# 512 weight columns as the moving side, k outermost, in the output projection and the second feed-forward product of a two-layer hybrid block

## The chip, the cores and the metric

The kernel runs on one core of one Trainium2 chip. The metric is the time of one execution in device microseconds (us).

## The reference, cut to what matters

Two layers work on 256 latent tokens `x` and 256 context tokens `xc`, with 1024 features. In each layer three token mixers (gated linear attention, differential attention, latent attention) share one input projection and are merged with gates into `y`; then come an output projection, a residual with a layer norm, and a SwiGLU feed-forward with another residual and norm. The context tokens are needed in layer 0 only. What matters here:

```
y = sum over branches of sigmoid(gate) * (branch @ w_branch)
y = y @ w_out                                   # 1024 x 1024
x = layer_norm(ALPHA * x + g1 * y) * ln1_g + ln1_b
h = layer_norm(x) * (1 + sc2) + sh2
gate, up = split(h @ ffn_w_in)                  # 1024 x 5632
f = (silu(gate) * up) @ ffn_w_out               # 2816 x 1024
x = layer_norm(ALPHA * x + g2 * f) * ln2_g + ln2_b
```

The shifts, scales and gates (sh, sc, g; six per layer) come from `silu(c) @ w_mod[l]`, which the kernel computes in steps between its other work.

## The kernel before, in words

All matrices are float32. To get float32 accuracy from TensorE, each operand is split into a rounded high part and a remainder, and one product takes three matmuls (mm3, lines 233 to 236): high by high, then the two mixed ones. A weight tile is loaded into a `raw` slot of up to 1024 elements a partition (load, line 181, on SP's queue; four slots), and split (line 198) in pieces of 512 elements a partition: ScalarE writes the high part (line 212), VectorE the remainder (line 213). Both go into `wh` and `wl`, three slots each, or into `wo`, 33 slots, where a tag is given and the weights are held. Loads and splits have high priority in the planner.

A planner orders each engine's instructions: it simulates the program with a cost model and takes, by priority, what is ready; program order gives the priority. On the chip each engine then follows that fixed order and waits on semaphores.

Tokens stand in tiles of 128, i = 0 and 1 latent, 2 and 3 context. In layer 0, NT = 4 tiles, in the last layer NT = 2.

**The output projection** (lines 1164 to 1185). The merged mixer output XM has eight tiles M (features on partitions), made by merge (line 967) in the order n = 0 to 7; hilo writes the high part on ScalarE (line 514) and the rest on VectorE (line 515). Tokens are taken in groups: (0, 1) and (2, 3) in layer 0, (0) and (1) in layer 1. Per group there are four blocks cb_ of 256 columns; per block and tile, tok_block goes through k = 0 to 7 with the token tile of XM as the stationary side and 256 weight columns as the moving side, 24 matmuls into one accumulator. The first group loads and holds all weights (16 splits), the second goes through the blocks backwards. After each block and tile proj_res (line 1157) multiplies by the gate row (line 1159), adds to the residual (line 1160) and takes statistics (line 1162), all on VectorE. After a group, residual (line 980) and modulate (line 374) make X2, by VectorE, TensorE transposes (line 384) and ScalarE (line 388); mods_until forces outstanding modulation steps. Just before, gate_rows (line 354) fetches the gate row on ScalarE's queue (line 410), which has to wait until the row's store (line 331) has landed.

**The feed-forward** (lines 1190 to 1261). hidden makes one of 22 tiles u, features on partitions, from ffn_w_in. In layer 0 this is done in two rounds, tiles 0 to 11 and 12 to 21 (RND = 12), and the first NLAT = 4 tiles of the first round are made for tokens 0 to 255 before tokens 256 to 511. After each round the second product adds into the residual: four blocks cb_ of 256 columns, per block an accumulator per token tile, k (here f) outermost in steps of four and the tiles inside. In layer 0's second round the tiles are taken in two parts, (0, 1) and (2, 3), each followed by residual and modulate for layer 1's X; the second part goes backwards through the blocks and keeps the weights of the last block (FHELD = 1). In layer 1 all 22 k are one round; its last block goes tile by tile, so that the first tile's residual and store run beside the second tile's matmuls.

**The modulation steps.** tick (line 338) counts; on every third tick it closes an open row and does one mod_step (line 289): a 512 KB load of w_mod, 16 matmuls, and with every fourth step a ScalarE copy of the row. wfeat, wtok, branch_part and mla_front_pass tick; the loop of the second product doesn't. Channel 5 of the last layer isn't taken by ticks.

Of the kernel before, what the change touches and what calls it, by code (L numbers as in the profile page):

```python
# [11 lines left out]
ALU = mybir.AluOpType  # L12
# [3 lines left out]
P = 128  # L16
D = 1024
KD = D // P
# [13 lines left out]
ALPHA = (2 * DEPTH) ** 0.25  # L32
# [11 lines left out]
def hybrid_block_kernel(  # L44
# [6 lines left out]
    nc = tc.nc  # L51
# [7 lines left out]
    def nm(s):  # L59
        uid[0] += 1  # L60
        return f"{s}_{uid[0]}"
# [3 lines left out]
    def T(shape, tag, dtype=F32):  # L65
        return sb.tile(shape, dtype, tag=tag, name=nm(tag), bufs=BUFS[tag])
# [3 lines left out]
    NEARLY = 8  # L70
    NCHAIN = 24
    NLAT = 4
    HELD = 4
    FHELD = 1
    RND = 12
    PB = dict(mm=8, s=2, t=2, o=6, md=1, first=15)

    def ps(tag, shape):
        return pp.tile(shape, F32, tag="ps_" + tag, name=nm("ps_" + tag), bufs=PB[tag])
# [34 lines left out]
    mm = nc.tensor.matmul  # L114
    act = nc.scalar.activation
    stt = nc.vector.scalar_tensor_tensor
    tt = nc.vector.tensor_tensor
# [21 lines left out]
    cur = []  # L139
# [58 lines left out]
    def split(v, tag=None):  # L198

        a, b = v.shape[1], v.shape[2]  # L200
        step = a if a * b <= 512 else a // 2
        hs, ls = [], []
        with tc.high_priority():
            for o in range(0, a, step):
                n = step * b
                if tag:
                    h, lo = T([P, 512], tag, F32R), T([P, 512], tag, F32R)
                else:
                    h = wp.tile([P, 512], F32R, tag="wh", name=nm("wh"), bufs=WB)
                    lo = wp.tile([P, 512], F32R, tag="wl", name=nm("wl"), bufs=WB)  # L210
                h, lo = [t[:, 0:n].rearrange("p (k c) -> p k c", c=b) for t in (h, lo)]
                nc.scalar.copy(h, v[:, o:o + step, :])  # L212
                tt(lo, v[:, o:o + step, :], r32(h), op=ALU.subtract)  # L213
                hs += [h[:, k, :] for k in range(step)]
                ls += [lo[:, k, :] for k in range(step)]
        return hs, ls

    def wtile(src, kt, n, tag=None):
        return split(load(src, kt, n), tag)
# [13 lines left out]
    def mm3(o, lh, ll, rh, rl, start, stop):  # L233
        mm(o, lh, rh, start=start, stop=False)  # L234
        mm(o, lh, rl, start=False, stop=False)  # L235
        mm(o, ll, rh, start=False, stop=stop)  # L236
# [13 lines left out]
    def wtok(src, tag=None):  # L250

        tick()
        tick()
        return [wtile(src[512 * j:512 * j + 512, :], 4, 256, tag) for j in range(2)]

    def tok_block(o, ws, X, t0, c0, c1):

        k = 0
        for wh, wl in ws:
            for j in range(len(wh)):  # L260
                mm3(o, X[k][0][:, t0:t0 + P], X[k][1][:, t0:t0 + P], wh[j][:, c0:c1], wl[j][:, c0:c1],
                    k == 0, k == KD - 1)
                k += 1
# [74 lines left out]
    def tick():  # L338
        ticks[0] += ticking[0]
        if ticking[0] and ticks[0] % ticks[1] == 0:  # L340
            if mod_open:
                mod_close()
            if mod_queue and (mod_now or mod_queue[0] < (DEPTH - 1, 5, 0)):
                mod_step()
# [690 lines left out]
    X, copied, ahead = first_X()  # L1035
# [29 lines left out]
    for l in range(DEPTH):  # L1065
# [10 lines left out]
        g = keep([P, 6])  # L1076
# [5 lines left out]
    for l in range(DEPTH):  # L1082
        last = l == DEPTH - 1
        TQ = L if last else L + LC
        NT = TQ // P
        if l:
            X = Xn
# [61 lines left out]
        XM = [pair("M", TQ) for n in range(KD)]  # L1149
# [5 lines left out]
        gw = [gate_rows(l, 2, s) for s in range(NT // 2)]  # L1155

        def proj_res(i, po, c0, gw, r, a, st=None):
            tmp = T([P, 512], "rt")[:, 0:256]
            tt(tmp, po, gw[i // 2][c0 // 512][:, c0 % 512:c0 % 512 + 256], op=ALU.mult)
            stt(r[:, c0:c0 + 256], r[:, c0:c0 + 256], a, tmp, op0=ALU.mult, op1=ALU.add)  # L1160
            if st is not None:
                nc.vector.bn_stats(st[:, c0 * 6 // 256:c0 * 6 // 256 + 6], r[:, c0:c0 + 256])

        X2 = new_X(TQ)
        groups = [(0,), (1,)] if last else [(0, 1), (2, 3)]
        wo = {}
        st = {i: small(24) for i in range(NT)}
        for g in groups:
            for cb_ in range(4) if g is groups[0] else (3, 2, 1, 0):

                if cb_ in wo:
                    ws = wo[cb_]
                else:
                    held = g is groups[0] and cb_ >= 4 - (4 if last else HELD)
                    ws = wtok(w_out[l, :, 256 * cb_:256 * cb_ + 256], "wo" if held else None)
                    if held:
                        wo[cb_] = ws
                for i in g:
                    po = ps("mm", [P, 256])
                    tok_block(po, ws, XM, P * i, 0, 256)  # L1180
                    proj_res(i, po, 256 * cb_, gw, cur[i], ALPHA, st[i])
            mods_until(l, 4)
            for i in g:
                residual(l, i, cur[i], G1, B1, st[i])
                modulate(cur[i], i, l, 3, X2)
        mods_until(l, 5)
        gw2 = [gate_rows(l, 5, s) for s in range(NT // 2)]
# [14 lines left out]
        for lo_f, hi_f in (((0, RND), (RND, 22)) if TQ == 512 else ((0, 22),)):  # L1202
            u = {f: pair("u", TQ) for f in range(lo_f, hi_f)}
            jobs = [(f, 0, TQ) for f in range(lo_f, hi_f)]
            if lo_f == 0 and TQ == 512:
                jobs = [(f, a, a + 256) for a in (0, 256) for f in range(NLAT)] + jobs[NLAT:]
            for f, a, b in jobs:
                hidden(f, a, b, *u[f])
            final = hi_f == FT
            parts = [range(NT)] if not final or last else [range(0, 2), range(2, 4)]  # L1210
            if final:
                st = {i: small(24) for i in range(NT)}
                if not last:
                    mods_until(l + 1, 1)
            held = {}
            for part in parts:
                for cb_ in range(4) if 0 in part else (3, 2, 1, 0):
                    tags = [t for t in ("mm", "t", "s", "o") for _ in range(PB[t])][4 * (cb_ % 2):]
                    pos = {i: ps(tags[n], [P, 256]) for n, i in enumerate(part)}

                    keeps = len(parts) > 1 and cb_ >= 4 - FHELD
                    ws = held.setdefault(cb_, {}) if keeps else {}

                    def ffn_out(f0, i, tag="wo" if keeps else None):
                        kt = min(4, hi_f - f0)
                        if f0 not in ws:
                            ws[f0] = wtile(ffn_w_out[l, P * f0:P * (f0 + kt), 256 * cb_:256 * cb_ + 256], kt, 256, tag)
                        wh, wl = ws[f0]
                        for f in range(f0, f0 + kt):
                            mm3(pos[i], u[f][0][:, P * i:P * i + P], u[f][1][:, P * i:P * i + P],  # L1230
                                wh[f - f0], wl[f - f0], f == lo_f, f == hi_f - 1)

                    steps = range(lo_f, hi_f, 4)
                    if last and cb_ == 3:

                        for i in part:
                            for f0 in steps:
                                ffn_out(f0, i, "wo")
                    else:
                        for f0 in steps:  # L1240
                            for i in part:
                                ffn_out(f0, i)
                    for i in part:
                        proj_res(i, pos[i], 256 * cb_, gw2, cur[i], 1.0 if lo_f else ALPHA,
                                 st[i] if final else None)
                if not final:
                    continue
                for i in part:
                    residual(l, i, cur[i], G2, B2, st[i])
                    if last:  # L1250
                        for j in range(2):
                            q = nc.sync if j else nc.scalar
                            q.dma_start(out[0, P * i:P * i + P, 512 * j:512 * j + 512], cur[i][:, 512 * j:512 * j + 512])
                    else:
                        if i == 0:
                            Xn = new_X(512)
                        if i < 2:
                            mid = tc.dram_tile([P, D], F32, name=f"mid{i}")
                            nc.scalar.dma_start(mid, cur[i])
                            tok[i] = mid  # L1260
                        modulate(cur[i], i, l + 1, 0, Xn)
# [53 lines left out]
```

## Time and profile before

| | |
|---|---|
| median of 3 runs | 2120.98 us (2118.11 to 2122.21) |
| profiled execution, its own time | 2119.53 us |
| its span in the trace | 2117.7 us |
| mean granted TensorE clock | 0.992 |
| busy: TensorE matmul, VectorE, ScalarE, GpSimd | 97%, 69%, 51%, 5% of the span |
| from HBM | 263.79 MB, 126 GB/s over the span |

The page gives busy time by engine over the whole span; matmuls are pipelined, so their busy times overlap, and what one costs in a stream is read from start to start. The page's chain, followed back from the last instruction, lies on TensorE for 77% of the span, on VectorE for 12% and on ScalarE for 5%.

### The profile page before, as it was taken

The numbers are of one execution on the slowest core, as the hardware profiler recorded it, in microseconds if no ns is written. First come the engines' busy times: TensorE is split into PE (matmuls) and PEld (weight loads), VectorE is DVE, ScalarE is ACT, GpSimd is POOL, SyncE is SP. The second block draws the span as 40 slices with busy tenths as digits, with TensorE's granted clock in tenths as the row PEclk, the third lists the DMA queues.
The fourth block names the chain that finished last, engine by engine and source line by source line (L and its number), as shares of the span: only waits on it lengthen the run. The fifth ranks groups of instructions, "written<-read, shape, count | busy, mean of one in ns | idle before, by whom it ended". The sixth has DMA issues, their size and how long they took to land.

```text
span 2117.7 us, 36478 instructions
## 1 busy us (share of the span) xinstructions
PE 2052.3 (97%) x14103; PEld 1808.8 (85%) x14103; DVE 1461.3 (69%) x3240; ACT 1073.1 (51%) x2495; POOL 98.2 (5%) x187
## 2 busy tenths in 40 slices
PE   7999999999999999899999999999999999998998
PEld 4888887887878788798899889988988988998998
DVE  4599758778478766685443348598577888785655
ACT  3755446666465642344321233765466676644452
POOL 0001001111000000010000000000011000000000
PEclk9999999999999999999999999999999999998999
DMA  9332333332322344646334346533434333668653
GB/s 292 100 90 80 116 85 113 89 107 71 101 72 75 82 140 124 183 120 182 95 98 137 114 125 188 149 94 115 142 90 141 108 114 87 177 203 212 167 176 115
DMA packets 349271, 268.30 MB, mean 127 GB/s; under 512 B 19932, under 2 KB 316520, under 8 KB 349096
## 3 DMA queue, kind: packets, MB, share of 16 engines
q1 hardware_dynamic: 335632, 252.22, 41.4%
q10 hardware_dynamic: 13464, 13.74, 2.2%
q8 instruction: 111, 1.82, 0.4%
q14 instruction: 64, 0.52, 0.1%
HBM read 263.79 MB, written 2.12 MB: 126 GB/s over the span
## 4 chain that ended last, share of the span: by engine, by line
PE 77%; DVE 12%; ACT 5%; issue 2%; POOL 2%; DMA 1%; ACTq 0%; DVEq 0%; POOLq 0%; SPq 0%
PE ps_mm L234 18%; PE ps_mm L235 18%; PE ps_mm L236 18%; PE ps_s L234 3%; PE ps_s L236 3%; PE ps_s L235 3%; POOL store L178 2%; DVE wl L213 2%; PE ps_md L299 2%; PE ps_s L682 1%; ACT rt L483 1%; PE ps_s L509 1%; PE ps_s L510 1%; PE ps_o L786 1%; ACT wh L212 1%
## 5 line engine op out<-in xcount | busy, mean ns | idle before, releaser
L213 DVE TENSOR_TENSOR wl<-raw,wh 128x512 fp32r<-128x512 f32 (+2 forms) x719 | 468.4, 674 | 143.1 <-ACT wh L212 70.7
L212 ACT CAST wh<-raw 128x512 fp32r<-128x512 f32 (+2 forms) x719 | 416.4, 611 | 234.7 <-PE ps_mm L235 128.8
L234 PE MATMUL ps_mm<-X,wh 128*128 128x512 f32 (+1 forms) x1264 | 438.9, 347 | 0.0
L236 PE MATMUL ps_mm<-X,wl 128*128 128x512 f32 (+1 forms) x1264 | 434.2, 344 | 0.0
L235 PE MATMUL ps_mm<-XL,wh 128*128 128x512 f32 (+1 forms) x1264 | 434.1, 343 | 0.0
L234 PEld LDWEIGHTS ps_mm<-X,wh 128*128 128x128 f32 x1264 | 241.3, 191 | 30.4 <-issue 4.7
L236 PEld LDWEIGHTS ps_mm<-X,wl 128*128 128x128 f32 x1264 | 240.9, 191 | 24.8
L235 PEld LDWEIGHTS ps_mm<-XL,wh 128*128 128x128 f32 x1264 | 241.2, 191 | 23.6
L235 PE MATMUL ps_mm<-wl,X 128*128 128x256 f32 (+1 forms) x544 | 157.3, 293 | 0.8 <-DVE wl L213 0.7
L236 PE MATMUL ps_mm<-wh,XL 128*128 128x256 f32 (+1 forms) x544 | 156.2, 292 | 0.0
L234 PE MATMUL ps_mm<-wh,X 128*128 128x256 f32 (+1 forms) x544 | 153.2, 295 | 0.0
L178 POOL TENSOR_TENSOR store<-store 128x1 f32<-128x1 f32 x112 | 76.3, 682 | 1636.8 <-DVE store L177 1613.3
L234 PE MATMUL ps_s<-X,wh 128*128 128x256 f32 (+1 forms) x384 | 126.0, 328 | 5.2 <-ACT wh L212 5.2
L236 PE MATMUL ps_mm<-wh,u 128*128 128x256 f32 x444 | 125.8, 283 | 0.0
L235 PE MATMUL ps_mm<-wl,u 128*128 128x256 f32 x444 | 125.6, 283 | 0.0
L234 PE MATMUL ps_mm<-wh,u 128*128 128x256 f32 x444 | 125.6, 283 | 0.0
L236 PE MATMUL ps_s<-X,wl 128*128 128x256 f32 (+1 forms) x384 | 125.1, 326 | 0.2 <-DVE wl L213 0.2
L235 PE MATMUL ps_s<-XL,wh 128*128 128x256 f32 (+1 forms) x384 | 124.9, 325 | 0.0
L234 PE MATMUL ps_mm<-Y,wh 128*128 128x512 f32 (+1 forms) x352 | 119.7, 340 | 0.1
L236 PE MATMUL ps_mm<-Y,wl 128*128 128x512 f32 (+1 forms) x352 | 118.8, 337 | 0.0
L235 PE MATMUL ps_mm<-Y,wh 128*128 128x512 f32 (+1 forms) x352 | 118.7, 337 | 0.0
L724 ACT ACTIVATE e<-ps_s,store 128x512 f32<-128x512 f32 (+1 forms) x144 | 88.4, 618 | 38.2 <-DVE store L722 37.1
(306 smaller groups left out, 4484.7 us busy)
## 6 DMA issues: line engine op xcount, KB each, us to landing
raw<-in_w_in_dram SPq DMA_DIRECT2D x144, 512.0 KB, 4.5
raw<-in_w_mod_dram SPq DMA_DIRECT2D x96, 512.0 KB, 4.2
raw<-in_ffn_w_in_dram SPq DMA_DIRECT2D x96, 512.0 KB, 5.5
raw<-in_w_branch_dram SPq DMA_DIRECT2D x48, 512.0 KB, 4.9
raw<-in_ffn_w_out_dram SPq DMA_DIRECT2D x46, 512.0 KB, 3.6
raw<-in_w_out_dram SPq DMA_DIRECT2D x16, 512.0 KB, 4.9
raw<-in_w_in_dram SPq DMA_DIRECT2D x16, 448.0 KB, 3.4
v<-grow ACTq DMA_DIRECT2D x12, 256.0 KB, 6.7
```

The lines of the kernel that those rows point to most:

```text
L178: nc.gpsimd.tensor_tensor(o, o, mhalf, op=ALU.pow)
L212: nc.scalar.copy(h, v[:, o:o + step, :])
L213: tt(lo, v[:, o:o + step, :], r32(h), op=ALU.subtract)
L234: mm(o, lh, rh, start=start, stop=False)
L235: mm(o, lh, rl, start=False, stop=False)
L236: mm(o, ll, rh, start=False, stop=stop)
L299: mm(pm[32 * g:32 * g + 32, :], cst[:, 2 * j + k, :], v[:, k, P * g:P * g + P], start=(j == 0 and k == 0), stop=(j == 3 and k == 1))
L483: act(qw[a:a + 32, :], pl[b:b + 32, :], AF.Copy, scale=f)
L509: mm(o, qs[m][:, q], ks[m][:, k], start=start, stop=False)
L510: mm(o, qs[2 + m][:, q], ks[m][:, k], start=False, stop=stop)
L682: mm(pa[:, i, :], kx[:, P * i:P * i + P], qx[:, P * j:P * j + P], start=True, stop=True)
L724: act(e, pscore, AF.Exp, bias=mx, accum_out=s)
```

## The change

The output projection takes 512 columns at a time. In the first group k is outermost over both halves of the columns: one accumulator per tile and half, so four in layer 0 and two in layer 1, and the residual work of all of them follows the last k. The second group goes half by half, second half first, with the held weights. The second feed-forward product takes 512 columns at a time as well, k outermost, with one accumulator per tile; in layer 0's second round the second half's weights are held for the second token part. In layer 1 the first half goes in one block of 512 columns, the second half in two blocks of 256, the last of them tile by tile as before. The new loader wide fetches two k tiles at a time and ticks once for each such pair. The values of the attention (wtok, tok_block) stay at 256 columns.

```diff
+    def wide(src, kt, tag=None):
+
+        for k in range(0, kt, 2):
+            tick()
+            n = min(2, kt - k)
+            wh, wl = wtile(src[P * k:P * (k + n), :], n, src.shape[-1], tag)
+            for j in range(n):
+                yield k + j, wh[j], wl[j]
+
+    def wide_block(pos, ws, X, kt, k0=0):
+
+        for k, wh, wl in ws:
+            for i in pos:
+                xh, xl = X[k0 + k]
+                mm3(pos[i], xh[:, P * i:P * i + P], xl[:, P * i:P * i + P], wh, wl, k == 0, k == kt - 1)
...
         def proj_res(i, po, c0, gw, r, a, st=None):
-            tmp = T([P, 512], "rt")[:, 0:256]
-            tt(tmp, po, gw[i // 2][c0 // 512][:, c0 % 512:c0 % 512 + 256], op=ALU.mult)
-            stt(r[:, c0:c0 + 256], r[:, c0:c0 + 256], a, tmp, op0=ALU.mult, op1=ALU.add)
+            n = po.shape[-1]
+            tmp = T([P, 512], "rt")[:, 0:n]
+            tt(tmp, po, gw[i // 2][c0 // 512][:, c0 % 512:c0 % 512 + n], op=ALU.mult)
+            stt(r[:, c0:c0 + n], r[:, c0:c0 + n], a, tmp, op0=ALU.mult, op1=ALU.add)
             if st is not None:
-                nc.vector.bn_stats(st[:, c0 * 6 // 256:c0 * 6 // 256 + 6], r[:, c0:c0 + 256])
+                for c in range(c0, c0 + n, 256):
+                    nc.vector.bn_stats(st[:, c * 6 // 256:c * 6 // 256 + 6], r[:, c:c + 256])
...
         for g in groups:
-            for cb_ in range(4) if g is groups[0] else (3, 2, 1, 0):
-
-                if cb_ in wo:
-                    ws = wo[cb_]
-                else:
-                    held = g is groups[0] and cb_ >= 4 - (4 if last else HELD)
-                    ws = wtok(w_out[l, :, 256 * cb_:256 * cb_ + 256], "wo" if held else None)
-                    if held:
-                        wo[cb_] = ws
-                for i in g:
-                    po = ps("mm", [P, 256])
-                    tok_block(po, ws, XM, P * i, 0, 256)
-                    proj_res(i, po, 256 * cb_, gw, cur[i], ALPHA, st[i])
+
+            pos = [{i: ps("mm", [P, 512]) for i in g} for _ in range(2)]
+            if g is groups[0]:
+                for both in zip(*[wide(w_out[l, :, 512 * j:512 * j + 512], KD, "wo") for j in range(2)]):
+                    wo.append(both)
+                    for j in range(2):
+                        wide_block(pos[j], both[j:j + 1], XM, KD)
+            else:
+                for j in (1, 0):
+                    wide_block(pos[j], [both[j] for both in wo], XM, KD)
+                    for i in g:
+                        proj_res(i, pos[j][i], 512 * j, gw, cur[i], ALPHA, st[i])
+            if g is groups[0]:
+                for j in range(2):
+                    for i in g:
+                        proj_res(i, pos[j][i], 512 * j, gw, cur[i], ALPHA, st[i])
             mods_until(l, 4)
...
+            def ffn_cols(c0, n, tiles, ws):
+                pos = {i: ps("mm", [P, n]) for i in tiles}
+                wide_block(pos, ws, u, kt, lo_f)
+                for i in tiles:
+                    proj_res(i, pos[i], c0, gw2, cur[i], 1.0 if lo_f else ALPHA, st[i] if final else None)
+
+            def fw(c0, n, tag=None):
+                return wide(ffn_w_out[l, P * lo_f:P * hi_f, c0:c0 + n], kt, tag)
+
             for part in parts:
...
+                if not final:
+                    for c0 in (0, 512):
+                        ffn_cols(c0, 512, part, fw(c0, 512))
+                    continue
+                if last:
+
+                    for c0, n in ((0, 512), (512, 256)):
+                        ffn_cols(c0, n, part, fw(c0, n))
+                    ws = list(fw(768, 256, "wo"))
                     for i in part:
+                        ffn_cols(768, 256, (i,), ws)
+                elif 0 in part:
+
+                    ffn_cols(0, 512, part, fw(0, 512))
+                    ws = list(fw(512, 512, "wo"))
+                    ffn_cols(512, 512, part, ws)
+                else:
+                    ffn_cols(512, 512, part, ws)
+                    ffn_cols(0, 512, part, fw(0, 512))
```

## Rows read from the trace of the kernel before

**Rows 1.** The page: the span, and busy time by engine with shares.

```profile
span 2117.7 us, 36478 instructions
...
PE 2052.3 (97%) x14103; PEld 1808.8 (85%) x14103; DVE 1461.3 (69%) x3240; ACT 1073.1 (51%) x2495; POOL 98.2 (5%) x187
```

**Rows 2.** Busy time by stretch: its length, engines with counts, granted clock, DMA share, GB/s.

```profile
869.75:903.05 33.30, 27.74 (x230) 26.46 (x227) 22.07 (x45) 10.77 (x20) 0.89 (x1) 0.90 0.67 200
903.05:928.98 25.93, 25.41 (x211) 24.90 (x210) 22.08 (x58) 9.13 (x22) 3.12 (x5) 1.00 0.01 2
1073.05:1142.26 69.21, 69.21 (x578) 69.07 (x576) 27.56 (x55) 15.25 (x27) 0.00 (x0) 1.00 0.28 85
1256.97:1317.13 60.16, 59.62 (x498) 59.30 (x497) 49.80 (x108) 28.45 (x58) 3.25 (x4) 1.00 0.56 174
1874.52:1899.62 25.10, 24.66 (x202) 24.10 (x201) 22.21 (x53) 7.52 (x18) 1.65 (x2) 1.00 0.49 168
1899.62:1911.66 12.04, 5.82 (x140) 4.69 (x139) 9.29 (x22) 4.07 (x11) 1.54 (x2) 0.85 1.02 275
2046.72:2110.24 63.52, 63.52 (x530) 63.32 (x528) 36.93 (x70) 22.34 (x41) 0.99 (x1) 1.00 0.43 137
```

**Rows 3.** Timeline of TensorE, first and last of 135 narrow and 68 wide matmuls.

```profile
1099.81 0.28 PE L235 MATMUL ps_mm<-wl,u 128*128 128x256 f32 x1
...
1115.89 0.28 PE L234 MATMUL ps_mm<-wh,u 128*128 128x256 f32 x1
...
1160.76 0.40 PE L234 MATMUL ps_s<-X,wh 128*128 128x512 f32 x1
...
1175.99 0.39 PE L235 MATMUL ps_s<-XL,wh 128*128 128x512 f32 x1
```

**Rows 4.** Timeline of TensorE in layer 0's first projection group; idle time before in brackets.

```profile
874.63 0.39 PE L234 MATMUL ps_mm<-wo,M 128*128 128x256 f32 x1 [2.46 <-ACT M L514]
...
879.09 0.58 PE L234 MATMUL ps_mm<-wo,M 128*128 128x256 f32 x1 [2.80 <-ACT M L514]
```

**Rows 5.** Timeline of ScalarE in the same stretch.

```profile
860.60 0.61 ACT L212 CAST wo<-raw 128x512 fp32r<-128x512 f32 x1
...
870.02 0.62 ACT L212 CAST wo<-raw 128x512 fp32r<-128x512 f32 x1 [8.80 <-DMA grow<-store]
...
878.42 0.62 ACT L514 CAST M<-acc 128x512 fp32r<-128x512 f32 x1 [1.81 <-DVE acc L976]
```

**Rows 6.** Busy time by stretch, columns as in rows 2: two stretches after a gap.

```profile
879.50:884.10 4.60, 4.60 (x23) 4.60 (x23) 2.47 (x6) 2.27 (x4) 0.00 (x0) 0.50 1.16 313
...
1911.60:1918.30 6.70, 6.64 (x29) 6.39 (x30) 3.91 (x9) 3.06 (x8) 0.00 (x0) 0.50 1.14 280
```

**Rows 7.** Groups of VectorE's instructions, 869 to 930 us: busy us, mean ns, idle before.

```profile
L213 DVE TENSOR_TENSOR wo<-raw,wo 128x512 fp32r<-128x512 f32 x11 | 7.4, 685 | 10.1 <-ACT wo L212 10.1
L1159 DVE TENSOR_TENSOR rt<-ps_mm,v 128x256 f32<-128x256 f32 x16 | 6.7, 416 | 9.4 <-PE ps_mm L236 9.4
L1162 DVE BATCH_NORM_STATS2 store<-A 128x6 f32<-128x256 f32 x15 | 6.3, 420 | 0.3
...
L985 DVE SCALAR_TENSOR_TENSOR A<-A,store,e 128x512 f32<-128x512 f32 x6 | 4.3, 743 | 0.0
```

**Rows 8.** Groups by shape, whole span: the matmuls of the modulation steps.

```profile
L299 PE MATMUL ps_md<-raw,store 128*32 128x128 f32 x1280 | 55.7, 280 | 0.0
```

**Rows 9.** Timelines of VectorE and TensorE: last X remainders, first matmul on later tokens.

```profile
920.41 0.69 DVE L393 TENSOR_TENSOR XL<-k,X 128x512 fp32r<-128x512 f32 x1
...
954.38 0.69 DVE L393 TENSOR_TENSOR XL<-k,X 128x512 fp32r<-128x512 f32 x1
...
956.94 0.39 PE L234 MATMUL ps_mm<-X,wh 128*128 128x256 f32 x1
...
1346.32 0.69 DVE L393 TENSOR_TENSOR XL<-k,X 128x512 fp32r<-128x512 f32 x1 [0.99 <-ACT X L392]
```

**Rows 10.** The page: DMA issues, KB each and us to landing.

```profile
raw<-in_ffn_w_out_dram SPq DMA_DIRECT2D x46, 512.0 KB, 3.6
```

More of the change, by code (lines that the diff above doesn't have):

```diff
@@ L72, in hybrid_block_kernel @@
     NLAT = 4
-    HELD = 4
-    FHELD = 1
     RND = 12
@@ L1161, in proj_res @@
             if st is not None:
-                nc.vector.bn_stats(st[:, c0 * 6 // 256:c0 * 6 // 256 + 6], r[:, c0:c0 + 256])
+                for c in range(c0, c0 + n, 256):
+                    nc.vector.bn_stats(st[:, c * 6 // 256:c * 6 // 256 + 6], r[:, c:c + 256])
         X2 = new_X(TQ)
         groups = [(0,), (1,)] if last else [(0, 1), (2, 3)]
-        wo = {}
+        wo = []
         st = {i: small(24) for i in range(NT)}
         for g in groups:
-            for cb_ in range(4) if g is groups[0] else (3, 2, 1, 0):
-                if cb_ in wo:
-                    ws = wo[cb_]
-                else:
-                    held = g is groups[0] and cb_ >= 4 - (4 if last else HELD)
-                    ws = wtok(w_out[l, :, 256 * cb_:256 * cb_ + 256], "wo" if held else None)
-                    if held:
-                        wo[cb_] = ws
-                for i in g:
-                    po = ps("mm", [P, 256])
-                    tok_block(po, ws, XM, P * i, 0, 256)
-                    proj_res(i, po, 256 * cb_, gw, cur[i], ALPHA, st[i])
+            pos = [{i: ps("mm", [P, 512]) for i in g} for _ in range(2)]
[13 more added lines that the diff above has]
+                        proj_res(i, pos[j][i], 512 * j, gw, cur[i], ALPHA, st[i])
@@ L1209, in hybrid_block_kernel @@
             final = hi_f == FT
+            kt = hi_f - lo_f
             parts = [range(NT)] if not final or last else [range(0, 2), range(2, 4)]
@@ L1214, in hybrid_block_kernel @@
                     mods_until(l + 1, 1)
-            held = {}
-            for part in parts:
[L1217 to L1242, printed above, removed]
-                    for i in part:
[L1244 to L1247, printed above, removed]
```

## The prediction

> **What bounds the kernel now.** I read the page first. TensorE's matmuls are busy for 2052.3 of 2117.7 us, VectorE for 1461.3, ScalarE for 1073.1 [rows 1]. So TensorE has the path nearly everywhere, and the questions are what a matmul costs there and where TensorE still waits. The table by stages answers the second [rows 2]. The second feed-forward product of layer 0 runs in two stretches, 69.21 us with TensorE busy for all of it and 60.16 us with 59.62 busy; that of layer 1 takes 63.52 us, all busy. The output projection differs: the first token group of layer 0 takes 33.30 us with 27.74 busy at a granted clock of 0.90, the second group 25.93 us with 25.41 busy. In layer 1 the projection takes 25.10 us, but there VectorE is busy for 22.21 of them, and a stretch of 12.04 us with only 5.82 of matmul follows.
>
> Busy time of pipelined matmuls overlaps, so I take a matmul's price from start to start. From 1099.81 to 1115.89 us, 134 matmuls of 256 columns follow each other: 0.1200 us each. From 1160.76 to 1175.99, 67 of 512 columns: 0.2273 each [rows 3]. Two narrow ones cost 0.2400, one wide one 0.2273.
>
> The gap in the first group is next. TensorE waits 2.46 and 2.80 us for the casts into M at line 514 [rows 4]. ScalarE makes them late: after a weight cast at 860.60 it does nothing for 8.80 us, held by the store of the modulation row, and makes the last M only at 878.42 [rows 5]. The clock falls after that gap: at 879.50 to 884.10 it is granted 0.50, the 1.2 GHz level, and 23 matmuls fill 4.60 us [rows 6].
>
> **The change, part by part.**
>
> *Fewer matmuls.* By the loops, lines 1180 and 1230 issue 2160 matmuls of 256 columns: 576 in the projection (6 tiles x 4 blocks x 24), 1584 in the second product (66 per tile and block; 4 tiles x 4 blocks and 2 x 4). All but the last two blocks of layer 1 (264) pair up: 1896 become 948. Each pair saves 0.2400 - 0.2273 = 0.0127 us, in all 12.0 us. The 96 pairs in layer 1's projection (1.2 us) I don't count: VectorE is nearly full there [rows 2], the tail behind it is VectorE's, and a faster TensorE meets it earlier. That leaves 10.8 us. For layer 1's projection I take 0, with bounds of 2 us lost and 1.2 won.
>
> This price comes from 512-column matmuls whose moving side is features; here it is weights. In the rows the difference of 0.0127 is the part of a matmul that doesn't grow with its columns. The Trainium skill (TensorE: Matmul & The Clock Gate, section "Wait — 56ns, not 53.3ns?") puts that fixed part at about 2.5 ns for back-to-back matmuls at 2.4 GHz, which speaks against the change. By that rule 948 fewer matmuls would save an estimated 2.4 us instead of 12.0; the rows disagree with it here, where every matmul also loads new weights.
>
> *The order over k.* Before, one accumulator goes through k = 0 to 7, so the first tile needs the late M[6] and M[7] after 18 matmuls (2.2 us). After, 12 wide matmuls (2 halves x 2 tiles x 3) share each k: M[6] is needed 72 x 0.2273 = 16.4 us after the start at 869.75, at 886.1, and M[7] at 888.9. The last M is there before 880 [rows 5]. So the wait goes. What is late next would be the split weights, two splits per k: each split feeds 1.36 us of matmuls and costs 0.685 on VectorE [rows 7] and about as much on ScalarE. Four raw slots hold eight splits, 10.9 us of cover. The price of the wait with its slow clock: 33.30 - 192 x 0.1200 - 2 modulation steps of 0.70 (55.7 us over 80 steps [rows 8]) = 8.9 us. Bounds: 0, if the planner's order keeps the wait, and 8.9; I take 8.9, since nothing in the new order asks for the late tiles early.
>
> *Residual work in a burst.* proj_res now comes for all blocks at the end of a group. For one 512 block and tile VectorE does a multiply and a multiply-add (0.74 each, taken from the 512-wide row of line 985) and two statistics of 0.42 [rows 7], issued a little closer: about 1.9 us, against three operations of 0.42 each, 1.0 to 1.3 us, for a 256 block. Layer 0's first group thus leaves four such blocks (7.5 us) behind its last matmul where one narrow block remained, so 6.5 us more. X2 of that group was ready 18.0 us after the group's end (903.05 to the end of the row at 920.41), used from 928.98 on; now it comes after 24.5, and the second group, shortened to about 24.5, ends then too. Loss about 1 us. X2 of the second group was ready 26.1 us after 928.98 and needed at 956.94, 1.9 us of slack [rows 9]; the burst adds 2.7 us and some backlog. Loss about 2. For both: 3 us, bounds 0 and 8. At the end of layer 0 both tiles of the second part end together with wide blocks, 1.7 us more of VectorE work ahead of the last X cast, which already ended at 1347.01 with the gate product on its heels [rows 9]: loss 1.5, bounds 0 and 4. In layer 1's final block the order stays tile by tile at 256 columns, so the end of the kernel costs the same.
>
> *Ticks moved.* The new wide() ticks once per pair of k; the old second product did not tick. 6 + 6 + 15 ticks in layer 0, a modulation step every third: 9 steps move from layer 1's mixer into the product, each with 16 matmuls, a 512 KB load on SP's queue and, every fourth, a ScalarE copy; one modulation row's store on ScalarE's queue moves too. 9 x 0.70 = 6.3 us of TensorE work changes places. Since TensorE is 97% busy all over [rows 1], nearly all comes back where it is taken; what filled gaps there is lost. I take 1 us, bounds 0 and 6.3. The loads are covered: DMA is at 0.28 and 0.56 of its time in those stretches [rows 2].
>
> *Costed at nothing.* Holding half of the columns instead of a quarter drops 5 splits (3.4 us of VectorE) in layer 0's last stretch, beside TensorE's work, which hides it now and would hide it still. Reads carry the same bytes in rows twice as long; layer 1's last 512 columns take twice as many, half-sized loads on SP's queue, hidden by four raw slots; if that cover is gone, TensorE stalls by up to the landing of a load, 3.6 us at 512 KB [rows 10]. Four accumulators of 512 columns take four of the tag mm's eight slots; a hand-over needs the first of them 0.7 us after its last matmul, which VectorE can meet while it is 40% busy [rows 2].
>
> **The sum**: -10.8 - 8.9 + 3 + 1.5 + 1 = -14.2 us. The profiled run took 2119.53 us for a span of 2117.7, 1.45 below the median of 2120.98. So 2105.3 against that run, 2106.8 against the median.
>
> **Rivals.**
> *A, the wait stays in another place.* ScalarE's 8.80 us remain in any case [rows 5]; if the planner, which doesn't know of them, runs the splits after instead of before them, TensorE waits for weights instead of M. For it: only the splits before 861 are safe. Against it: the eight raw splits come back at one per 0.6 us from 870 on. Time: 2106.8 + 8.9 = 2115.7.
> *B, the change doesn't do what it says: a wide matmul with weights as moving side saves next to nothing per pair.* Against it: the flat 0.1200 and 0.2273 [rows 3]. If only a fifth of the price holds, the sum loses 0.8 x 10.8 = 8.7: 2115.5. The Trainium skill's fixed part, cited above, would lead to nearly this.
> *C, slower: the residual chain takes TensorE's place.* Its price stands in layer 1, where nothing covers it: after the projection 12.04 us with 5.82 of matmul [rows 2], then 29 matmuls in 6.70 us at a clock of 0.50 [rows 6], which would take 3.5 us at 0.1200: 9.4 us. If the two tails of layer 0's projection and the one into layer 1 became like that, 28.2 us stand against gains of 18.7 (the sum without its tail terms): 2106.8 - 4.5 + 28.2 = 2130.5. It decides from 18.7 us, two full tails. For it: slack of 1.9 us and VectorE busy for 22.08 of 25.93 us in the second group [rows 2]. Against: hidden blocks of the first tokens give 23 us of cover in two of the places, early gates in the third.
>
> **How the numbers follow.** Forecast 0.66, with a range of its own from 2100 (no tail or tick cost, 14.2 + 5.5 won) to 2114 (tails at 8 and 4 us). A 0.15, B 0.05, C 0.07; 0.07 is left for a new order elsewhere that takes back the gain to within 0.2% (4.2 us, about what a measurement of this kernel can tell from no change). The range reaches from 2100 to 2117, which takes in A and B and leaves out C and half of the rest. Faster: the forecast with most of A and B, less what lands above 2116.7: 0.82. Within: 0.10. Slower: C and a little: 0.08.
>
> **What would show it.** The two stretches of the second product in layer 0 at about 0.947 of their matmul time plus moved steps (69.21 to 65.5 + 2.8), wide starts 0.227 apart; the first group near 23.3 us with no half clock at 880; the 8.80 us on ScalarE still there; transposes for X2 waiting on VectorE for 1 to 3 us behind each group; layer 1's 12.04 us about as long. I am wrong if wide starts lie 0.24 apart, if a wait of over 5 us stands in or behind the projection of layer 0, or if layer 1's mixer grows by more than the steps it lost.

## The result, and the profile after

The changed kernel takes 2108.86 us (median of 4 runs, 2106.58 to 2110.05) beside 2121.60 for the kernel before (4 runs, 2118.11 to 2122.68): a ratio of 0.9945, 95% interval 0.9932 to 0.9957. The forecast was 2106.8, in a range of 2100 to 2117. The profiled execution took 2110.05 us.

The page of the kernel after, its span and the busy times [rows 1]:

```profile
span 2108.2 us, 34491 instructions
...
PE 2041.8 (97%) x13155; PEld 1756.4 (83%) x13155; DVE 1454.2 (69%) x3175; ACT 1076.3 (51%) x2490; POOL 98.0 (5%) x187
```

Busy time by stretch of the kernel after, columns as in rows 2: the two groups of layer 0's projection, the two rounds of its second product, layer 1's mixer, its projection with the tail behind it, and its second product:

```profile
872.01:895.77 23.76, 23.76 (x135) 18.86 (x131) 13.53 (x22) 9.86 (x18) 0.00 (x0) 1.00 0.91 257
895.77:919.87 24.10, 23.97 (x116) 19.67 (x114) 22.36 (x54) 8.08 (x20) 3.89 (x4) 1.00 0.08 22
...
1064.55:1133.28 68.73, 68.73 (x358) 55.63 (x355) 23.96 (x40) 13.99 (x26) 0.00 (x0) 1.00 0.48 146
...
1247.47:1309.47 62.00, 60.91 (x340) 48.34 (x338) 44.33 (x85) 25.25 (x53) 3.51 (x4) 1.00 0.60 187
1309.47:1869.04 559.57, 540.92 (x3940) 494.52 (x3938) 435.90 (x1039) 357.78 (x878) 28.79 (x58) 1.00 0.42 122
1869.04:1892.30 23.26, 23.01 (x107) 18.57 (x105) 18.53 (x40) 5.89 (x14) 1.53 (x2) 1.00 0.18 58
...
1892.30:1906.53 14.23, 6.97 (x142) 5.41 (x141) 11.96 (x29) 6.36 (x17) 1.53 (x2) 0.77 1.28 278
...
2038.80:2100.58 61.78, 61.78 (x398) 56.40 (x396) 37.80 (x67) 22.95 (x41) 0.99 (x1) 1.00 0.44 138
```

The same view of the kernel before for the stretch that the rows ahead of the prediction leave out, layer 1's mixer:

```profile
1317.13:1874.52 557.39, 545.08 (x4089) 498.47 (x4087) 432.94 (x1039) 355.43 (x878) 29.76 (x58) 1.00 0.44 128
```

Against [rows 2] the first group falls from 33.30 us to 23.76, all busy, at a granted clock of 1.00 where it was 0.90. That is most of the gain. The second group falls from 25.93 to 24.10 and layer 1's product from 63.52 to 61.78. Layer 0's product falls little in its first round (69.21 us, 69.78 with the modulation step behind it, to 68.73) and grows in its second (60.16 to 62.00): nine modulation steps now stand in the two rounds, four and five. The mixer of layer 1, which lost these nine steps, did not get shorter: 557.39 before, 559.57 after, and TensorE's idle time in it (length less busy) rose from 12.3 to 18.7 us. The difference of 2.2 us in length alone says little: executions that issue this stretch in one and the same order take 557.39 to 560.51 us. Layer 1's projection falls from 25.10 to 23.26, and the stretch behind it grows from 12.04 to 14.23: together 37.14 and 37.49, no gain. The next stretch, up to layer 1's second product, falls from 135.06 us to 132.27, which no term of the forecast has.

Timeline of TensorE in the kernel after, first and last of 71 wide matmuls with weights as the moving side:

```profile
1099.33 0.39 PE L233 MATMUL ps_mm<-wl,u 128*128 128x512 f32 x1
...
1115.23 0.39 PE L234 MATMUL ps_mm<-wh,u 128*128 128x512 f32 x1
```

70 intervals in 15.90 us are 0.2271 us each, the price that [rows 3] showed for features.

Timeline of ScalarE around the first group of the kernel after:

```profile
862.86 0.62 ACT L210 CAST wo<-raw 128x512 fp32r<-128x512 f32 x1
...
873.98 0.62 ACT L210 CAST wo<-raw 128x512 fp32r<-128x512 f32 x1 [10.50 <-DMA grow<-store]
...
877.76 0.62 ACT L528 CAST M<-acc 128x512 fp32r<-128x512 f32 x1 [0.44 <-DVE acc L990]
...
884.21 0.62 ACT L528 CAST M<-acc 128x512 fp32r<-128x512 f32 x1 [1.56 <-DVE acc L990]
```

ScalarE's hold is still there, 10.50 us instead of 8.80 [rows 5], and the last M comes at 884.83, later against the group's start than before. TensorE doesn't notice: 12 matmuls share each k, so M[7] is asked for 84 x 0.2271 = 19.1 us after 872.01, at 891.1.

### The profile page after: what moved, and what is told of

Its sections match the earlier page's. It is cut to its first block, busy times and chain, and to the rows that moved or that the text cites. A ratio compares the mean times of both kernels' runs of the same rounds, so it can differ in the third digit from the quotient of the medians.

```text
span 2108.2 us, 34491 instructions
## 1 busy us (share of the span) xinstructions
PE 2041.8 (97%) x13155; PEld 1756.4 (83%) x13155; DVE 1454.2 (69%) x3175; ACT 1076.3 (51%) x2490; POOL 98.0 (5%) x187
## 4 chain that ended last, share of the span: by engine, by line
PE 78%; DVE 12%; ACT 5%; POOL 2%; issue 2%; DMA 1%; DVEq 0%; ACTq 0%; SPq 0%; POOLq 0%
PE ps_mm L232 18%; PE ps_mm L233 18%; PE ps_mm L234 18%; PE ps_s L232 3%; PE ps_s L233 3%; PE ps_s L234 3%; POOL store L176 2%; DVE wl L211 2%; PE ps_md L313 2%; PE ps_s L696 1%; PE ps_s L523 1%; PE ps_s L524 1%; ACT rt L497 1%; PE ps_o L800 1%; ACT e L738 1%
## 5 line engine op out<-in xcount | busy, mean ns | idle before, releaser
L211 DVE TENSOR_TENSOR wl<-raw,wh 128x512 fp32r<-128x512 f32 (+1 forms) x709 | 467.4, 674 | 319.7 <-issue 90.9
L210 ACT CAST wh<-raw 128x512 fp32r<-128x512 f32 (+1 forms) x709 | 410.9, 610 | 327.1 <-PE ps_mm L233 187.3
L233 PEld LDWEIGHTS ps_mm<-wl,X 128*128 128x128 f32 x544 | 103.9, 191 | 4.0 <-DVE wl L211 3.0
L234 PEld LDWEIGHTS ps_mm<-wh,XL 128*128 128x128 f32 x544 | 103.9, 191 | 0.8
L232 PEld LDWEIGHTS ps_mm<-wh,X 128*128 128x128 f32 x544 | 100.7, 191 | 2.6 <-issue 1.4
```

## The experiments

**The parts, and the width.** Two kernels make half of the change; a third keeps it all and issues each 512-column matmul as two of 256 columns into the same accumulator:

```diff
-                mm3(pos[i], xh[:, P * i:P * i + P], xl[:, P * i:P * i + P], wh, wl, k == 0, k == kt - 1)
+                th, tl = xh[:, P * i:P * i + P], xl[:, P * i:P * i + P]
+                w = wh.shape[-1]
+                for o in range(0, w, 256):
+                    c = slice(o, o + 256)
+                    mm3(pos[i][:, c], th, tl, wh[:, c], wl[:, c], k == 0 and o == 0, k == kt - 1 and o + 256 == w)
```

Projection alone (second product as before). Expected: 

> The new output projection with the old second product. Theory 1 (the projection's gain is the wait of 8.9 us that goes, plus the price of fewer matmuls; the layer-1 mixer lost its 7 us because modulation steps were moved out of it): the two groups of layer 0 take about 24 us each, the mixer stretch of layer 1 keeps its 557 us, the whole about 2121.6 - 13 = 2108.5 us, as fast as the full change. Theory 2 (the mixer is slower because the planner's order of everything behind the projection changed): the mixer stretch is long here too, 560 us or more with its 19 steps, and the whole is about 2113 us.

Second product alone (projection as before). Expected: 

> The new second product with the old output projection. Theory 1: 8.4 us fewer in the three product stretches, against 7 us lost in the layer-1 mixer, and the wait of 2.46 and 2.80 us with the half clock behind it still in layer 0's first group: about 2120 us, within 0.2% of the kernel before. Theory 2, for which the mixer's loss belongs to the changed projection: 2121.6 - 8.4 = 2113 us with a mixer of 552 us (557 less the 9 steps).

Narrow matmuls in the new order. Expected: 

> The changed kernel, in which each matmul of 512 weight columns is issued as two of 256, the second half following the first in the same bank; loads, splits and the order over k stay. Theory 1 (0.0127 us per pair): 948 more pairs of instructions, starts 0.120 apart, 9 to 12 us more than the changed kernel, 2118 to 2121 us, and no wait in layer 0's projection. Rival (the gain is the order alone, and a wide matmul costs what two narrow ones cost): within 2 us of 2108.9 us.

Measured against 2122.78: projection alone 2109.30 (0.9939, 0.9927 to 0.9952), second product alone 2120.78 (0.9989, 0.998 to 0.9998), narrow matmuls 2121.11 (0.9993, 0.9984 to 1.0002). Five stretches of the narrow kernel, the two groups, the two rounds of layer 0's product and layer 1's product (columns as in rows 2):

```profile
869.96:894.74 24.78, 24.78 (x230) 24.12 (x227) 13.63 (x22) 9.74 (x18) 0.00 (x0) 1.00 0.90 249
894.74:920.11 25.37, 25.22 (x212) 24.84 (x210) 23.03 (x55) 8.08 (x20) 3.89 (x4) 1.00 0.02 4
...
1064.93:1137.20 72.27, 72.27 (x647) 71.06 (x643) 24.07 (x40) 13.98 (x26) 0.00 (x0) 1.00 0.46 139
1251.34:1316.11 64.77, 63.64 (x579) 61.66 (x578) 44.68 (x85) 25.28 (x53) 3.50 (x4) 1.00 0.57 179
...
2047.77:2111.29 63.52, 63.52 (x530) 63.31 (x528) 36.20 (x66) 22.23 (x41) 0.99 (x1) 1.00 0.42 134
```

The new order takes the wait away without the width: 24.78 us against 33.30. The width is worth 1.0 us there, 3.5 and 2.8 in the product's rounds, 1.3 in the second group and 1.7 in layer 1's product, 10.3 us outside layer 1's projection. And the projection alone gives all that the whole change gives: the second product's width is eaten up by something that came with it. The projection alone has the time of its first theory and, with 560.51 us, the long mixer of its second. That length is no sign for the second: TensorE's order there is that of the kernel before, and two of the kernels below with the same order take 557.91 and 560.04 us.

**The steps moved.** The change, but the second product doesn't tick:

```diff
-    def wide(src, kt, tag=None):
+    def wide(src, kt, tag=None, ticks=True):
...
-            tick()
+            if ticks:
+                tick()
...
-                return wide(ffn_w_out[l, P * lo_f:P * hi_f, c0:c0 + n], kt, tag)
+                return wide(ffn_w_out[l, P * lo_f:P * hi_f, c0:c0 + n], kt, tag, False)
```

Expected: 

> The changed kernel, whose loader doesn't tick in the second product, so that no modulation step moves. Theory 1 (the steps filled gaps in the layer-1 mixer, and their work in the product is lost): the product's two stretches in layer 0 fall by 1.7 and 2.9 us, the mixer is back at 19 steps and 557 to 560 us, the whole about 2104 us. Theory 3 (the mixer's extra 7 us come from the burst of residual work at the end of layer 0, which makes layer 1's first X late): the mixer takes the steps back on top, 565 us, and the whole stays at 2108.9 us.

Measured 2106.89 us (0.9925, 0.9912 to 0.9937), between the two expectations. Its interval overlaps that of the change (0.9932 to 0.9957), so by the times alone the cost of the steps is not clear of noise here; the pair with the next edit, on one chip, shows it (2101.49 to 2104.07 us with the steps moved, 2098.40 to 2101.12 without).

**The end of layer 0.** The change, but the last token part takes the fresh half of the columns first and the held half last, tile by tile:

```diff
-                    ffn_cols(512, 512, part, ws)
                     ffn_cols(0, 512, part, fw(0, 512))
+                    for i in part:
+                        ffn_cols(512, 512, (i,), ws)
```

Expected: 

> The kernel after, but in layer 0's last token part the first half of the columns comes first (fresh weights) and the second half last, with the held weights and tile by tile (30 matmuls of 512 columns each), so that one tile's residual work runs beside 6.8 us of the other tile's matmuls. Theory 1 (layer 1's mixer starts late because the residual work of both tiles of the last part comes in a burst): the stalls over 0.3 us in the mixer's first 70 us fall from 4.5 us towards the 1.3 to 1.9 of the kernels with the narrow second product, in all 2 to 4 us less: 2105 to 2107. Rival (the differences in the mixer come from the planner's other order there, or are scatter between runs): the mixer stays at 557 to 563 us and the time within 1.5 us of the kernel after, 2107.5 to 2110.

Both edits together. Expected: 

> Two edits on the kernel after: the second product does not tick (the modulation steps go back to layer 1's mixer), and layer 0's last part goes tile by tile in its last half. Theory 1 (both cost time and add up): 2103 to 2105, against about 2107 with the ticks' edit alone. Rival (the order of tiles is worth nothing): 2106 to 2108.

Measured on one chip beside 2122.15: 2103.40 us (0.9909, 0.9894 to 0.9924) and 2099.57 us (0.9894, 0.988 to 0.9907). Both are below what was expected, and faster than the change. The last remainder X of the next layer in the timeline of VectorE, first in the kernel after, then with the tiles last:

```profile
1340.89 0.69 DVE L407 TENSOR_TENSOR XL<-k,X 128x512 fp32r<-128x512 f32 x1 [1.15 <-ACT X L406]
```

```profile
1332.60 0.69 DVE L407 TENSOR_TENSOR XL<-k,X 128x512 fp32r<-128x512 f32 x1 [0.97 <-ACT X L406]
```

and that kernel's second round and mixer (columns as in rows 2):

```profile
1248.19:1308.70 60.51, 60.51 (x339) 48.49 (x338) 48.21 (x95) 26.65 (x54) 4.69 (x5) 1.00 0.68 208
1308.70:1865.88 557.18, 540.75 (x3939) 494.38 (x3938) 431.96 (x1029) 356.63 (x876) 27.74 (x57) 1.00 0.41 117
```

The last X starts 29.2 us after the product's end before [rows 2, 9], 31.4 after the change and 23.9 with the tiles last. The mixers of the projection alone, of no ticks and of both edits:

```profile
1306.71:1867.22 560.51, 547.27 (x4089) 498.52 (x4088) 435.38 (x1039) 358.64 (x880) 29.90 (x58) 1.00 0.44 129
...
1300.89:1864.49 563.60, 547.40 (x4088) 498.71 (x4087) 436.77 (x1042) 359.15 (x880) 29.68 (x58) 1.00 0.45 130
...
1299.79:1860.94 561.15, 547.18 (x4087) 498.53 (x4086) 433.66 (x1034) 357.75 (x878) 29.14 (x58) 1.00 0.43 125
```

TensorE's idle time in layer 1's mixer, length less busy time of the same view, sorts the kernels:

| steps in the mixer | old product | new product | new, tiles last |
|---|---|---|---|
| 19 | 12.3 (before), 13.2 (projection alone) | 16.2 (no ticks) | 14.0 (both edits) |
| 10 | | 18.7 (after), 18.3 (product alone) | 16.4 |

Each comparison comes out alike: taking nine steps away leaves 2.5 us more idle (13.97 to 16.43, and 16.20 to 18.65), the new product 3.0 to 3.9 us, the tiles last give back 2.2 in either row. Before and the projection alone issue this stretch in the same order and differ by 0.9 in idle time and by 3.1 in length; so idle time, not length, is compared here. By the ratios the tiles last are worth about 7 us; the profiles show 1.5 at the product's end (nothing without ticks, 57.68 and 57.62) and 2.4 in the mixer. Another 3.1 us lie in layer 1's tail (146.50 us to 143.35, from the projection's end to the product). That this part belongs to the edit is not shown: four kernels with it take 143.0 to 146.6 us there, three without it and with the same projection 145.3 to 147.3, all with spells at half clock, 10.2 to 13.7 us in sum.

**The wait.** The change with k innermost in the first projection group, at full width:

```diff
-                for both in zip(*[wide(w_out[l, :, 512 * j:512 * j + 512], KD, "wo") for j in range(2)]):
-                    wo.append(both)
-                    for j in range(2):
-                        wide_block(pos[j], both[j:j + 1], XM, KD)
+                wo = list(zip(*[list(wide(w_out[l, :, 512 * j:512 * j + 512], KD, "wo")) for j in range(2)]))
+                for j in range(2):
+                    for i in g:
+                        wide_block({i: pos[j][i]}, [both[j] for both in wo], XM, KD)
```

Expected: 

> The kernel after, but in the first projection group of each layer the halves of the columns come one after the other, with k innermost (tile by tile, 24 matmuls of 512 columns into one accumulator); the width stays 512. Theory 1 (the order over k removed the wait for the late M): the first tile now needs M[6] and M[7] about 4 us after the group's start, and all splits of the first half within 5.5 us, so a wait of 3 to 8 us comes back in layer 0's first group, most likely with granted clock below 1.00 behind it: the group 27 to 33 us instead of 23.75, in all 2112 to 2119. Rival (the wait went for another reason: the wider accumulators, the loads in another order, the planner): the group stays at 23.8 to 25 us, in all 2107 to 2110.

Measured 2120.61 us (0.9993, 0.9984 to 1.0001), a little above the expectation. Its first group (columns as in rows 2):

```profile
874.46:906.73 32.27, 25.93 (x114) 20.55 (x115) 20.29 (x37) 8.57 (x16) 0.99 (x1) 0.80 0.67 178
```

and the gap in it on TensorE's timeline:

```profile
883.30 1.08 PE L313 MATMUL ps_md<-raw,store 128*32 128x128 f32 x16 [6.34 <-DMA raw<-in_w_mod_dram]
```

A wait of 6.34 us with a slow clock is back, so the width alone doesn't take it away; the order does, for the narrow kernel had no wait either. But it ends here with the load of a modulation step, not with M: the size of the wait came out as expected, its cause didn't. SP's queue issues that load only at 875.55, after ScalarE was held for 11.63 us up to 873.21. Three kernels then asked the kernel before what makes its M late. Two edits on channel 2's gate row:

```diff
-        gates(2, range(8))
+        gates(2, range(4))
+        if not last:
+            mods_until(l, 2)
+        gates(2, range(4, 8))
```

Expected: 

> The kernel before, with one edit in layer 0: the outstanding modulation steps of channel 2 are forced in the middle of the last branch's eight gates instead of behind them, so that the row's store starts earlier. Theory 1 (TensorE's wait in the first projection group was ScalarE's, held by that store's landing): ScalarE's 8.80 us become under 2, TensorE's waits of 2.46 and 2.80 us and the half clock behind them go, the group comes to 25 to 27 us from 33.3 and the whole to 2113 to 2116. Rival (M is late by VectorE or by the gates themselves): the group stays above 30 us and the time at 2120 to 2123.

```diff
-        return bcast_row(grow[l, ch][s], "v")
+        return bcast_row(grow[l, ch][s], "v", nc.gpsimd if ch == 2 else nc.scalar)
...
-    def bcast_row(src, tag):
+    def bcast_row(src, tag, q=nc.scalar):
```

Expected: 

> The kernel before, but the gate rows of channel 2 are fetched on GpSimd's queue instead of ScalarE's, so that ScalarE no longer stands behind the wait for the row's store. Theory 1 (the late M in layer 0's first projection group was ScalarE's, held for 8.80 us by that store; forcing the row earlier only moved this hold to an earlier place, 10.32 us long, with M as late as before): ScalarE's hold goes, M[6] and M[7] come 5 us or more earlier against the group's start, and the group comes to 25 to 28 us from 33.3, with the granted clock at 1.00: 2113 to 2117 in all. Rival (VectorE, or the gates' own matmuls, make M late): the group stays above 31 us and the whole at 2120 to 2124.

The latter with the two edits of above. Expected: 

> The kernel after with three edits: no ticks in the second product, the last half of layer 0's last part tile by tile, and the gate rows of channel 2 on GpSimd's queue. Theory 1 (k outermost already covers ScalarE's hold): layer 0's first group stays at 23.75 us and the whole within 2 us of the same kernel without the third edit, 2098 to 2101. Rival (ScalarE's hold still costs time with the new order, behind the group or in layer 1): 2092 to 2097.

Measured: 2124.95 us (1.0013, 1.0004 to 1.0022), the first group at 33.11; 2124.94 (1.0008, 0.9999 to 1.0017), at 34.87; with the two edits 2100.85 (0.9892, 0.9878 to 0.9905), at 23.76. The first kept the hold (10.32 us), only earlier. The second shows why neither could help; the DMA issues that touch the row, over layer 0's mixer:

```profile
L410 POOL DMA_DIRECT2D v<-grow x4: 546/549/739, 738.8 to 745.5; - x4
L410 ACTq DMA_DIRECT2D v<-grow x4: 338/476/666, 873.8 to 875.5; - x4
```

Channel 2's row is fetched at 738.8, long before. What holds ScalarE is the fetch of channel 5's row, needed only by the second product 200 us later; the planner puts it right behind that row's own store. So the last pair moves that fetch behind the last cast into X2:

```diff
+            last_x[:] = [getattr(ins, "ins", ins)]
...
-        gw2 = [gate_rows(l, 5, s) for s in range(NT // 2)]
+        with tc.issue_after(last_x[0]):
+            gw2 = [gate_rows(l, 5, s) for s in range(NT // 2)]
```

Here `ins` is modulate's cast into X.

On the kernel before, expected: 

> The kernel before, with one edit: the gate rows of channel 5 (needed by the second feed-forward product alone) are fetched after the last cast into X2 instead of as soon as their slots are free. By the order of ScalarE's queue it is this fetch, not that of channel 2, that stands behind the store at 858.49 and holds ScalarE for 8.80 us; so the two kernels that moved channel 2 could not take the hold away. Theory 1 (this hold made M late and so made the wait that the new order removes): ScalarE's hold goes, the first projection group of layer 0 comes to 25 to 28 us from 33.3 at a granted clock of 1.00, and the whole to 2112 to 2117. Rival (M is late by VectorE or by the gates' matmuls): the group stays above 31 us and the whole at 2120 to 2124.

With the two edits of above, expected: 

> The kernel after with three edits: no ticks in the second product, the last half of layer 0's last part tile by tile, and the fetch of channel 5's gate rows after the last cast into X2. Theory 1 (k outermost already covers ScalarE's hold): layer 0's first group stays at 23.75 us and the whole within 2 us of the same kernel without the third edit: 2098 to 2102. Rival (the hold still costs time in the new order): 2092 to 2097.

Measured 2124.79 us (1.001, 1.0002 to 1.0019), the first group at 35.83; and 2097.76 (0.9889, 0.9874 to 0.9904), at 23.76. ScalarE in the former:

```profile
868.53 0.62 ACT L517 CAST M<-acc 128x512 fp32r<-128x512 f32 x1 [1.45 <-DVE acc L979]
876.97 1.14 ACT L212 CAST wo<-raw 128x512 fp32r<-128x512 f32 x2 [7.82 <-DMA raw<-in_w_out_dram]
...
882.26 0.62 ACT L517 CAST M<-acc 128x512 fp32r<-128x512 f32 x1 [1.67 <-DVE acc L979]
```

and TensorE:

```profile
882.93 0.58 PE L234 MATMUL ps_mm<-wo,M 128*128 128x256 f32 x1 [8.27 <-ACT M L517]
```

The theory of the single cause falls. The store's hold is gone and M[6] is cast at 868.53, before the group starts. But then a weight cast that stands ahead of M[7] in ScalarE's order waits 7.82 us for its load, and M[7] comes as late as before. Behind the one hold stood another of the same length, and the order that doesn't ask for M[7] early escapes both. Why that load is late the trace shows in part. SP's queue first waits 7.7 us, up to 860.32, for a slot that a modulation step's matmuls hold. The load itself is issued at 864.02, 3.4 us behind the row's store at 860.61, and ends the wait at 876.97, about 13 us later; in the kernel before, the loads of w_out issued at 845.18 and 850.08, ahead of the store, land after 4.9 and 4.7 us. Busy time by stretch of the kernel with the late fetch, ahead of the store and while the load is on its way:

```profile
850.00:856.00 6.00, 6.00 (x28) 4.96 (x27) 3.90 (x7) 3.15 (x6) 0.00 (x0) 1.00 1.08 358
...
864.02:876.97 12.95, 10.64 (x70) 8.71 (x68) 4.92 (x8) 2.09 (x4) 0.00 (x0) 1.00 0.66 55
```

DMA moves 358 GB/s in the first and 55 in the second. The row's two stores, 4 KB each, pass as 2080 packets on a queue of their own between 860 and 877 us. So both holds may come from the small store, the first by its own landing and the second by the loads beside it; no run changed how the row is stored, so this isn't shown.

The last kernel is the fastest: 2097.76 us (2096.80 to 2102.24, 4 runs), 1.1% under the kernel before. Its third edit makes no difference that these runs can tell: 2099.57 stands beside it without a third edit, 2100.85 with the other one.

## Why the prediction was right

By its own steps, in us:

| term | predicted | shown |
|---|---|---|
| fewer matmuls | -10.8 | -10.3 (after against narrow matmuls) |
| order over k | -8.9 | -8.5, and -0.6 in the second group (narrow against before) |
| layer 1's projection | 0 (-1.2 to 2) | -1.8 there, 2.2 behind it |
| residual bursts in layer 0's projection | 3 (0 to 8) | 0.7 |
| tail at the end of layer 0 | 1.5 (0 to 4) | 3.0 to 3.9 in the mixer, about 0.5 ahead of it |
| steps moved | 1 (0 to 6.3) | 2.5 |

The terms shown add up to between -12.3 and -11.4; the medians differ by 12.7. The stretch ahead of layer 1's second product, 2.8 us shorter in the profile after, is in no row: kernels with the old projection take 132.9 to 136.9 us there, seven with the new one 128.8 to 133.1, with spells at half clock of different lengths, and whether that is the change's wasn't tested. That the forecast came within 2.1 us of the median is in part luck: the last three terms were put at 5.5 us and show 6.7 to 7.6, because the first was too high by 2.3 and the others too low by 2.0 to 2.9 and by 1.5.

**Fewer matmuls** was right in size: a pair was to cost 0.0127 us less as one, and with weights as the moving side it costs 0.0129 less from start to start (0.2400 - 0.2271), 0.0121 by the narrow kernel (10.3 us over 852 pairs). The Trainium skill's fixed part (TensorE: Matmul & The Clock Gate, section "Wait — 56ns, not 53.3ns?") gave an estimate of 2.4 us for all 948 pairs; the measured 10.3 for 852 of them decides against it here. **The order over k** was right for the reason given, that nothing asks for the late M early: the last M came even later, at 884.83, and TensorE didn't wait. The rival that the wait stays elsewhere is out, since the group is busy for 23.76 of 23.76 us. The step failed in naming what made M late: the hold on ScalarE was one of two, and taking it alone away gained nothing. **Layer 1's projection** is the case where the profile told most: VectorE was nearly full there [rows 2], and the faster TensorE met its tail earlier, to the microsecond: projection and tail together take 37.1 to 38.4 us in five kernels with the old projection and 37.5 in seven with the new one. The forecast that this tail stays "about as long" was wrong by the same 2.2 us.

Three terms were mis-sized within their bounds. **The residual bursts** were put at 3 us: X2's last remainder of the first group ends at 920.68, 24.9 us after that group's end (24.5 in the forecast), and the second group ends at 919.87, yet TensorE doesn't stop there, since its first matmuls on X2 take the first half of the features and the last remainder belongs to the second. The second tail costs waits of 0.46 and 0.22 us instead of 2. **The tail at layer 0's end** went the other way: the prediction counted VectorE's extra work (1.7 us; the last X is 2.2 us later) as the only delay, but the stretch behind it lost about twice that; that more than one product there stands behind X would explain it, and wasn't taken apart. **The steps** were argued from TensorE being 97% busy; in layer 1's mixer it idles 12 us, and steps stood in part of that idle time. Taken out, they gave back about 6.3 - 2.5 = 3.8 us (the mixers with and without them differ by 4.0); in the product, where TensorE stops for 1.1 us at most, they cost about all of their 6.3 (7.1 in one pair of kernels, 5.7 in the other). The sign that the prediction named for being wrong, the mixer growing, can't be decided by its length (2.2 us more, within the scatter of 3.1); what the runs show is that it didn't get 6.3 us shorter, and its idle time rose by 6.3. The slower rival (the residual chain in TensorE's place) had its mechanism at two of its three places, 0.7 us behind the second group and 3.5 to 4.4 at layer 0's end, against 9.4 each.

## What to carry to other kernels

Where an operand arrives piece by piece, put the loop over these pieces outermost, over several accumulators: here the last piece was then asked for 19.1 us after the stage's start, so that it could come at 12.8 us without a wait, whatever had delayed it; taking away one cause alone gained nothing. Wider moving sides save the fixed part of each matmul only where TensorE has the path, and a bigger block sends its residual work out in one burst, so a stage that others wait for had better end tile by tile. Filler work belongs where the engine idles, so look at idle time stage by stage before moving it into a stage that is full.

## What was not expected of the hardware

The granted clock differs between executions at places that the change doesn't touch. Busy time by stretch, first the kernel after, then the kernel before:

```profile
606.00:610.00 4.00, 4.00 (x12) 3.13 (x11) 2.69 (x6) 1.10 (x2) 0.00 (x0) 0.57 0.17 50
```

```profile
606.00:610.00 4.00, 4.00 (x19) 3.33 (x18) 2.03 (x4) 2.29 (x4) 0.00 (x0) 1.00 0.07 21
```

Up to layer 0's projection both give TensorE the same matmuls in the same order, yet after has a granted clock of 0.57 there and reaches the projection 2.26 us later (872.01 against 869.75); about 1.7 of the 2.26 arise between 587 and 633 us, where this spell lies. In the ten kernels with the same order up to there that point lies between 869.75 and 872.87 us, so a gain of 2 or 3 us is read from stretches and repeated runs and not from one span.
